# Branch moved to the fifth of eight expert pairs, gated-embedding products spaced evenly, one more weight tile, router products taken before LayerNorm

## The chip, the cores and the metric

One core of a Trainium2 chip runs the whole layer. The metric is the device time of one execution in microseconds, lower is better. Five engines work side by side, each on its own instructions in program order: TensorE (PE), VectorE (DVE), ScalarE (ACT), GpSimd (POOL), and SyncE (SP), which here issues every DMA.

## The reference, cut to what matters

One layer on 256 tokens of width 2048: a token-mixing part, a LayerNorm, a router, a mixture of 16 experts (two per token), a gated embedding, and a second LayerNorm. The part around the change is:

```python
x = _layer_norm(ALPHA * x + mix, ln1_g, ln1_b)
logits = xf @ router_w                      # 2048 x 16
affinity = sigmoid(logits); sel = affinity + router_bias
# best group of four experts, in it the best two
hb = silu(xb @ w_gate[e]) * (xb @ w_up[e]);  y = hb @ w_down[e]
ple = sigmoid(x @ ple_w_gate) * (p @ ple_w_proj)
x = _layer_norm(ALPHA * x + ffn + ple, ln2_g, ln2_b)
```

With LayerNorm written as x1 = (y - mean) * r, the logits are r * (y @ (g w)) - r * mean * (column sums of g w) + (column sums of b w). The changed router uses this form.

## The kernel before, in words

**Staging.** Everything is fp32 and every weight is read once. A pool of twelve tiles of 2 MB (128 x 4096 fp32, `big`, line 40) holds the weight stream and the large activations. `load_one` (line 127) issues one weight tile on SP; `prefetch` (line 142) issues as long as live tiles plus `state["reserve"]` stay below twelve, and `done` (line 152), called after the last product of a tile, frees that tile and calls `prefetch`. So a weight load waits on SP for the release of a tile, and SP issues in program order. `keep(n)` raises the reserve, `BR` takes a reserved tile for an activation. The small tiles come from a pool of five (`S`, line 55, 128 x 512 fp32); all of them carry one tag and are given out again in the order in which they came free.

**Order of the work.** The order is written out by hand. Short pieces of background work sit in a list `bg`; `pop_bg` (line 159) takes one after every second piece of a projection and one after every half tile of an expert product.

**Projections.** Until about 608 us each weight tile is split into a high and a low part (ACT line 264, DVE line 265) through four buffers, three pieces ahead of PE, and PE multiplies three times (line 283). The last of them are the four blocks of the output projection `wo` (line 510), each of 16 pieces. After each block DVE adds the residual (line 514) and takes LayerNorm statistics (line 515).

**Router.** After the last block: mean and deviation (lines 522 to 525, 553), a product of router weights and LayerNorm bias (line 565) and ten filler products `busy(10)` (line 567) on PE; then x1 is normalized in place by `norm_d` (DVE, line 557) and `norm_a` (ACT, line 561), turned by PE (line 578), copied out (lines 581, 583) and multiplied by the router weights (line 550). The logits are copied (line 601), turned (line 605), summed (line 608), and then come the sigmoid (line 611), the choice of experts (lines 613 to 648), the one-hot selection (line 676), the gather of the chosen rows (line 698) and the first expert product (line 790).

**Experts.** Eight pairs of experts, 64 places each. Each pair has phases A and B (8 tiles each, `inner`, line 806: gate and up products, line 790) and 0 and 1 (4 tiles each, `outer`, line 817: down products, line 797). `evac` (line 847) splits the result of an outer phase into four small tiles, yh on ACT and yl on DVE for each of two halves, and `scatter` (line 861) multiplies them by the selection and adds to `acc`. The scatters of phase 0 run as events after half tiles 1 to 4 of phase 1, and those of phase 1 in phase A of the next pair. The gathers for the next pair run as background, mostly in phase A.

**Gated embedding.** Eight products `ple(i)` (line 760) of 64 matmuls with one weight tile each, placed by the table `PLE` (line 31) after a phase of a pair. While one runs, PE releases no other tile.

**Branch.** `overflow` (line 927) holds a run-time branch (line 929) whose body, for experts with more than 64 tokens, is not entered with these inputs. It stands before phase A of the eighth pair. Two tiles are reserved for its body.

**Ends.** In the seventh pair the second LayerNorm's gain and bias are read into a tile `rows` (line 1010), spread over the partitions by two POOL broadcasts (lines 1026, 1027) into `gb2`, and also kept as two rows (line 1030). After the last expert product, line 1050 and following: statistics, six products of two rows with 512 columns (line 1072), a DVE operation for each (line 1073), and the stores.

Of the kernel before, what the change touches and what calls it, by code (L numbers as in the profile page):

```python
# [17 lines left out]
T = 256  # L18
# [12 lines left out]
PLE = [(2, "A"), (2, "1"), (3, "A"), (4, "A"), (4, "1"), (5, "A"), (6, "A"), (6, "B")]  # L31
# [3 lines left out]
def trunk(ctx, tc, I, out):  # L35
# [89 lines left out]
    wpt = C("wpt", [128, 2, 2, 256])  # L125

    def load_one():
# [8 lines left out]
        if key[0] == "ple":  # L136
            SP.dma_start(wpt[:, key[1] % 2], I["ple_w_proj"][key[1]])
# [63 lines left out]
    tail = C("tail", [128, 128])  # L201
    DVE.tensor_scalar(tail, jp, 0.0, None, op0=OP.is_le)
    capm = C("capm", [128, 128])
# [4 lines left out]
    ones = C("ones", [128, 128])  # L208
# [294 lines left out]
    rbias = C("rbias", [128, 1])  # L503
    DVE.memset(rbias, 0.0)
# [48 lines left out]
    DVE.scalar_tensor_tensor(lnm, lmv[:, :, 0], -1.0, lrs, op0=OP.mult, op1=OP.mult)  # L553

# [18 lines left out]
    for pr in range(8):  # L573
# [27 lines left out]
    DVE.tensor_scalar(lt[:, 0:256], rps[:, 0:256], rbias, None, op0=OP.add)  # L601
    busy(2)
    lg = AUX()
    for a in range(2):
# [4 lines left out]
                      op=OP.add)  # L609
    aff = r3("aff", 2, NE)  # L610
    ACT.activation(aff, logit, AF.Sigmoid)
    sel = r3("sel", 2, NE)
# [53 lines left out]
    long = {}  # L666
# [3 lines left out]
    hTs = [C(f"hT{k}", [128, 4, 128]) for k in range(2)]  # L670
    pT = C("pT", [128, 2, T])
    SP.dma_start(pT, I["pT"])
# [87 lines left out]
    def ple(i):  # L760
# [4 lines left out]
        for a in range(2):  # L765
            for c in range(2):
                PE.matmul(pw[:, a * 256:(a + 1) * 256], pT[:, c, a * 128:(a + 1) * 128], wpt[:, i % 2, c, :],
                          start=(c == 0), stop=(c == 1))
# [11 lines left out]
        if i == len(PLE) - 1:  # L780
            free()
            keep()
# [108 lines left out]
    rowc = C("rowc", [2, T])  # L891
# [35 lines left out]
    def overflow():  # L927
        most = nc.values_load(cmi[0:1, 0:1], min_val=0, max_val=T)
        with tc.If(most > CAP):
            with tc.For_i(0, NP, 1) as g:  # L930
# [5 lines left out]
                xg = B("og")[:, 0:2048].rearrange("p (c s) -> p c s", c=DC)  # L936
                with tc.For_i(1, T // CAP, 1):
                    DVE.tensor_scalar(ce[:, 0], ce[:, 0], -float(CAP), None, op0=OP.add)
                    P = Pm[:, 0]
                    onehot(P, ce[:, 0])  # L940
                    selection(P, ce[:, 1], 0, NP)
                    for f in gathers(P, xg):
                        f()
# [14 lines left out]
                    for k in range(2):  # L958
# [3 lines left out]
                        for f in scatters(evac(ps), 0, 1024 * k):  # L962
                            f()
                free(2)

    onehot(Pm[:, 0], pair_of(pos, 0))
    gather(Pm[:, 0], xgs[:, 0], 0)
    gather(Pm[:, 0], xgs[:, 0], 1)
    weights()
    bg.extend([lambda cp=cp: gather(Pm[:, 0], xgs[:, 0], cp) for cp in range(2, 8)])  # L970
    bg.append(lambda: selection(Pm[:, 0], pair_of(wA, 0), 0, 0))
    gb2 = rows = None
# [7 lines left out]
    for g in range(NP):  # L980
        xg, i = xgs[:, g % 2], g % 2
        following = []
        if g < NP - 1:
            P = Pm[:, 1 - i]
            following.append(lambda P=P, g=g: onehot(P, pair_of(pos, g + 1)))
            if g == 0:
                following.extend([lambda P=P, x=xgs[:, 1], cp=cp: gather(P, x, cp) for cp in range(8)])
            else:
                following.extend(gathers(P, xgs[:, 1 - i]))
# [8 lines left out]
        if g == 2:  # L998
            bg.extend([lambda q=q, a=a: residual(q, a) for q in range(4) for a in range(2)])
        if g == NP - 2:  # L1000
            keep()
        if g == NP - 1:
# [3 lines left out]
            keep(-2)  # L1006
            overflow()
        ps = inner("A", g, xg, events(back, 1))
        if g == NP - 2:
# [6 lines left out]
        ps = inner("B", g, xg, {3: lambda: turn_hidden(s, hTs[0])})  # L1016
        s = hidden(ps, g)
        ples(g, "B")
        if g == 0:
            bg.extend(following)  # L1020
# [3 lines left out]
        if g == NP - 2:  # L1024
            gb2 = BR("gb2")
            POOL.partition_broadcast(gb2[:, 0:2048], rows[0:1, 0:D], channels=128)
            POOL.partition_broadcast(gb2[:, 2048:2560], rows[0:1, 2 * D - 512:2 * D], channels=128)
# [3 lines left out]
            free()  # L1031
            keep()
# [31 lines left out]
    for a in range(2):  # L1064
        PE.matmul(ps[0:2, a * 128:(a + 1) * 128], cw[:, a, :], ident, start=True, stop=True)  # L1065
    ACT.activation(rowc, ps[0:2, 0:T], AF.Copy)  # L1066
# [3 lines left out]
    for n, (q, a) in enumerate((q, a) for q in range(3) for a in range(2)):  # L1070
        ps = (AUX, MM)[n % 2]()
# [67 lines left out]
```

## Time and profile before

| | |
|---|---|
| three timed runs, us | 1609.93, 1611.82, 1611.93 (median 1611.82) |
| the profiled execution, us | 1613.37 |
| its span from first to last instruction, us | 1611.7 |
| granted clock of TensorE, mean | 0.994 |
| busy share of the span | PE 97%, DVE 34%, ACT 25%, POOL 2% |
| moved by DMA | 540.08 MB, mean 335 GB/s |

The profiled execution lies 1.55 us above the median of the timed runs. A busy PE in these views is not PE at its peak, since the ends of matmuls are modelled; the share and rate of the DMA engines are those of the 16 engines together. "SPq" is the issuing side of SyncE and "PEq" that of TensorE. A granted clock of 1.00 is 2.4 GHz and one of 0.50 is 1.2 GHz.

### The profile page before, as it was taken

The numbers are of one execution on the slowest core, as the hardware profiler recorded it, in microseconds if no ns is written. First come the engines' busy times: TensorE is split into PE (matmuls) and PEld (weight loads), VectorE is DVE, ScalarE is ACT, GpSimd is POOL, SyncE is SP. The second block draws the span as 40 slices with busy tenths as digits, with TensorE's granted clock in tenths as the row PEclk, the third lists the DMA queues.
The fourth block names the chain that finished last, engine by engine and source line by source line (L and its number), as shares of the span: only waits on it lengthen the run. The fifth ranks groups of instructions, "written<-read, shape, count | busy, mean of one in ns | idle before, by whom it ended". The sixth has DMA issues, their size and how long they took to land. (4 is left out here: it accounts for less than half of the span.)

```text
span 1611.7 us, 17489 instructions
## 1 busy us (share of the span) xinstructions
PE 1571.3 (97%) x7226; PEld 910.5 (56%) x7226; DVE 546.9 (34%) x945; ACT 405.7 (25%) x714; POOL 37.8 (2%) x42
## 2 busy tenths in 40 slices
PE   8999999999999999999999999999999999998878
PEld 6888878888888885333334444533525533552323
DVE  5555575556565564022222112012011112101005
ACT  5455555455554442011111001001000101000000
POOL 0000000000000000000000000000000000000002
PEclk9999999999999999999999999999999999999998
DMA  9843453445546847999999999999999999999994
GB/s 383 346 157 111 182 205 147 178 160 207 186 180 263 336 188 274 416 428 427 427 428 425 414 426 429 382 428 428 427 428 427 418 429 427 427 427 389 416 429 197
DMA packets 43613, 540.08 MB, mean 335 GB/s; under 512 B 7172, under 2 KB 7172, under 8 KB 10758
## 3 DMA queue, kind: packets, MB, share of 16 engines
q1 hardware_dynamic: 43528, 538.91, 81.3%
q8 instruction: 58, 0.95, 0.3%
q14 instruction: 27, 0.22, 0.0%
HBM read 536.80 MB, written 2.10 MB: 334 GB/s over the span
## 5 line engine op out<-in xcount | busy, mean ns | idle before, releaser
L790 PE MATMUL mm<-w,xg 128*64 128x512 f32 x2048 | 467.7, 601 | 16.0 <-DMA w<-in_exp_w_dram 9.5
L283 PE MATMUL mm<-pc,xh 128*128 128x512 f32 x1152 | 362.9, 395 | 6.2 <-ACT pc L264 5.6
L265 DVE TENSOR_TENSOR pc<-w,pc 128x512 fp32r<-128x512 f32 x416 | 290.8, 709 | 199.6 <-ACT pc L264 196.9
L264 ACT ACTIVATE pc<-w 128x512 fp32r<-128x512 f32 x416 | 259.6, 630 | 234.0 <-DVE pc L265 179.7
L790 PEld LDWEIGHTS mm<-w,xg 128*64 128x64 f32 x2048 | 138.4, 137 | 277.1 <-issue 252.4
L797 PE MATMUL mm<-w,hT 128*64 128x512 f32 (+2 forms) x1088 | 236.2, 573 | 9.3 <-DMA w<-in_exp_d_last_dram 5.6
L283 PEld LDWEIGHTS mm<-pc,xh 128*128 128x128 f32 x1152 | 213.8, 189 | 51.8 <-ACT pc L264 6.0
L283 PE MATMUL mm<-pc,xl 128*128 128x512 f32 x576 | 225.4, 391 | 0.0
L797 PEld LDWEIGHTS mm<-w,hT 128*64 128x64 f32 x1088 | 72.5, 136 | 137.9 <-issue 127.4
L283 PEld LDWEIGHTS mm<-pc,xl 128*128 128x128 f32 x576 | 108.5, 188 | 22.9
L772 PE MATMUL mm<-w,x1T 128*128 128x256 f32 x512 | 112.0, 379 | 0.0
L772 PEld LDWEIGHTS mm<-w,x1T 128*128 128x128 f32 x512 | 97.2, 190 | 13.2
L834 DVE TENSOR_TENSOR s<-s,mm 128x256 f32<-128x256 f32 x32 | 13.3, 417 | 214.1 <-ACT s L833 214.1
L283 PE MATMUL mm<-pc,mixh 128*128 128x512 f32 x256 | 79.1, 390 | 0.0
L833 ACT ACTIVATE s<-mm 128x256 f32<-128x256 f32 x32 | 12.3, 384 | 235.1 <-PE mm L790 225.7
L873 DVE TENSOR_TENSOR acc<-acc,aux 128x512 f32<-128x512 f32 (+2 forms) x60 | 38.8, 650 | 94.4 <-PE aux L868 92.5
L855 ACT ACTIVATE yh<-mm 128x512 fp32r<-128x512 f32 (+1 forms) x32 | 18.5, 590 | 161.9 <-PE mm L797 161.9
L283 PEld LDWEIGHTS mm<-pc,mixh 128*128 128x128 f32 x256 | 47.9, 188 | 9.9
L283 PE MATMUL mm<-pc,mixl 128*128 128x512 f32 x128 | 49.8, 389 | 0.0
L856 DVE TENSOR_TENSOR yl<-mm,yh 128x512 fp32r<-128x512 f32 (+1 forms) x32 | 21.5, 682 | 82.1 <-ACT yh L855 81.9
L283 PE MATMUL mm<-pc,yax 128*128 128x512 f32 x192 | 44.2, 389 | 0.0
L283 PE MATMUL mm<-pc,obx 128*128 128x512 f32 x192 | 44.2, 389 | 0.0
(208 smaller groups left out, 835.0 us busy)
## 6 DMA issues: line engine op xcount, KB each, us to landing
w<-in_exp_w_dram SPq DMA_DIRECT2D x184, 2048.0 KB, 19.0
w<-in_w_in_dram SPq DMA_DIRECT2D x34, 2048.0 KB, 8.5
w<-in_w_o_dram SPq DMA_DIRECT2D x8, 2048.0 KB, 13.3
w<-in_ple_w_gate_dram SPq DMA_DIRECT2D x8, 2048.0 KB, 21.0
w<-in_exp_d_last_dram SPq DMA_DIRECT2D x7, 2048.0 KB, 39.1
w<-in_w_out_a_dram SPq DMA_DIRECT2D x4, 2048.0 KB, 8.1
w<-in_w_out_b_dram SPq DMA_DIRECT2D x4, 2048.0 KB, 7.9
w<-in_w_in_dram SPq DMA_DIRECT2D x3, 1024.0 KB, 10.9
```

Source lines behind the costliest of these rows:

```text
L264: ACT.activation(hi, w, AF.Copy)
L265: DVE.tensor_sub(lo, w, hi.bitcast(F32))
L283: PE.matmul(ps[a], l[:, c, as_], r, start=(first and n == 0), stop=(last and n == 2))
L772: PE.matmul(ps[:, a * 256:(a + 1) * 256], x1T[:, c, a * 128:(a + 1) * 128], w[:, c, :], start=(c == 0 and a == 0), stop=(c == DC - 1), ski ...
L790: PE.matmul(ps[k][es, :], x[:, es], w[:, e, k, :], start=(c == 0), stop=(c == DC - 1), skip_group_check=True, tile_position=(0, 64 * e))
L797: PE.matmul(p[es, 0:n], hTs[fc // 4][:, fc % 4, es], w[:, e, b * n:(b + 1) * n], start=(fc == 0), stop=(fc == 7), skip_group_check=True, t ...
L833: ACT.activation(s[:, ks], pg[:, ks], AF.Sigmoid)
L834: DVE.tensor_mul(s[:, ks], s[:, ks], pg[:, ks])
L855: ACT.activation(h, p[:, 0:n], AF.Copy)
L856: DVE.tensor_sub(l, p[:, 0:n], h.bitcast(F32))
L873: DVE.tensor_add(xb, xb, ps[:, 0:n])
```

## The change

Six parts. **The router** works on rows that are not normalized: x1 is turned right after the last block, the statistics of the last block and the deviation are taken meanwhile, and mean and deviation enter on the logits, two small DVE operations. The sums that this needs come from `column_sums`, background work in the fourth block: two products and two sums on DVE, one product on PE, a copy on DVE. The bias product and `busy(10)` go; x1 is normalized later, partly behind the logits. **The tiles:** the first pair's gathered rows move to memory of their own, so that eleven instead of ten tiles are free for weights in the router stage; the second gather buffer, the embedding's small weights, `pT` and `rowc` share one tile `late`, which is reserved in phase B of the first pair. **The embedding products** behind 3A, 5A and 6B go behind 3B, 5B and phase 1 of pair 6 (pairs counted from 0), so that 16 tiles lie between any two. **The branch** goes from before pair 7 to before pair 4, with one reserved tile. **The gain and bias** of the second LayerNorm are read without the tile `rows`: their last 512 columns go into small tiles `ends`, from which POOL spreads them; the two tiles of the split x1 are freed in pair 6. **At the end** a filler product follows each of the first five two-row products.

```diff
-PLE = [(2, "A"), (2, "1"), (3, "A"), (4, "A"), (4, "1"), (5, "A"), (6, "A"), (6, "B")]
+PLE = [(2, "A"), (2, "1"), (3, "B"), (4, "A"), (4, "1"), (5, "B"), (6, "A"), (6, "1")]
+OVER = 4
...
+            SP.dma_start(long["wp"][:, key[1] % 2], I["ple_w_proj"][key[1]])
...
+    red = C("red", [128, 2, NE])
+    rsb = C("rsb", [128, 2, NE])
     lst = C("lst", [128, 2, 4, 6])
     lmv = C("lmv", [128, 2, 2])
     lrs = C("lrs", [128, 2])
     lnm = C("lnm", [128, 2])
+    def column_sums():
+        rwb = S("rwb").rearrange("p (c e) -> p c e", c=DC)
+        for k, t in ((0, rwg), (1, rwb)):
+            DVE.tensor_tensor(t, rw, gc[:, k, :, None].to_broadcast([128, DC, 32]), op=OP.mult)
+            DVE.tensor_reduce(red[:, k], t.rearrange("p c e -> p e c")[:, 0:NE, :], axis=AX.X, op=OP.add)
+        ps = AUX()
+        PE.matmul(ps[:, 0:2 * NE], ones, red.rearrange("p k e -> p (k e)"), start=True, stop=True)
+        DVE.tensor_copy(rsb.rearrange("p k e -> p (k e)"), ps[:, 0:2 * NE])
+    def stats(i, a):
+        DVE.bn_stats(lst[:, a, i, :], x1[:, a, i * 512:(i + 1) * 512])
...
+        if i == 3:
+            bg.extend([None, column_sums])
...
-            DVE.bn_stats(lst[:, a, i, :], xb)
-        if i == 2:
-            DVE.tensor_tensor(rwg, rw, gc[:, 0, :, None].to_broadcast([128, DC, 32]), op=OP.mult)
+            if i < 3:
+                stats(i, a)
     free(3)
-    xgs = B("xg").rearrange("p (h c s) -> p h c s", h=2, c=DC)
+    xgs = [C("xg0", [128, DC, 128]), None]
     prefetch()
-    for a in range(2):
-        DVE.bn_aggr(lmv[:, a, :], lst[:, a, :, :])
-    DVE.tensor_scalar(lrs, lmv[:, :, 1], EPS, None, op0=OP.add)
-    POOL.tensor_tensor(lrs, lrs, half, op=OP.pow)
+    def scales():
+        for a in range(2):
+            DVE.bn_aggr(lmv[:, a, :], lst[:, a, :, :])
+        DVE.tensor_scalar(lrs, lmv[:, :, 1], EPS, None, op0=OP.add)
+        POOL.tensor_tensor(lrs, lrs, half, op=OP.pow)
...
-    rbp = AUX()
-    for c in range(DC):
-        PE.matmul(rbp[0:32, 0:1], rw[:, c, :], gc[:, 1, c:c + 1], start=(c == 0), stop=(c == DC - 1))
-    DVE.tensor_copy(rbias[0:32, :], rbp[0:32, 0:1])
-    busy(10)
-    norm_d(0, 0)
-    norm_a(0, 1)
-    norm_d(1, 0)
-    norm_a(1, 1)
...
-        if pr == 1:
-            norm_d(2, 0)
-            norm_a(2, 1)
-        if pr == 3:
-            norm_d(3, 0)
-            norm_d(3, 1)
-        if pr % 2 == 1 and pr > 1:
-            route_mm(pr - 3, xts[pr - 3])
+    for pr in range(8):
+        turn_raw(pr)
+        if pr in (1, 3):
+            stats(3, pr // 2)
+        if pr == 5:
+            scales()
+        if pr >= 2:
             route_mm(pr - 2, xts[pr - 2])
     route_mm(6, xts[6])
     route_mm(7, xts[7])
+    DVE.scalar_tensor_tensor(lnm, lmv[:, :, 0], -1.0, lrs, op0=OP.mult, op1=OP.mult)
+    for a in range(2):
+        DVE.scalar_tensor_tensor(red[:, a], rsb[:, 0], lnm[:, a:a + 1], rsb[:, 1], op0=OP.mult, op1=OP.add)
+    norm_d(0, 0)
+    for q, a in ((0, 1), (1, 0), (1, 1)):
+        norm_a(q, a)
...
-    DVE.tensor_scalar(lt[:, 0:256], rps[:, 0:256], rbias, None, op0=OP.add)
+    DVE.tensor_copy(lt[:, 0:256], rps[:, 0:256])
+    norm_d(2, 0)
...
+        DVE.scalar_tensor_tensor(logit[:, a], logit[:, a], lrs[:, a:a + 1], red[:, a], op0=OP.mult, op1=OP.add)
     aff = r3("aff", 2, NE)
     ACT.activation(aff, logit, AF.Sigmoid)
+    for q, a in ((2, 1), (3, 0), (3, 1)):
+        norm_a(q, a)
...
-    pT = C("pT", [128, 2, T])
-    SP.dma_start(pT, I["pT"])
+    hTs = [hT0, C("hT1", [128, 4, 128])]
+    def take_late():
+        t = BR("late")
+        xgs[1] = t[:, 0:2048].rearrange("p (c s) -> p c s", c=DC)
+        long["wp"] = t[:, 2048:3072].rearrange("p (k c f) -> p k c f", k=2, c=2)
+        long["pT"] = t[:, 3072:3584].rearrange("p (c t) -> p c t", c=2)
+        long["rowc"] = t[0:2, 3584:3840]
+        SP.dma_start(long["pT"], I["pT"])
...
-                xg = B("og")[:, 0:2048].rearrange("p (c s) -> p c s", c=DC)
+                xg, f = xgs[1 - OVER % 2], 1 - OVER % 2
...
+        if g == OVER - 1:
+            bg.extend([None] * 20 + [keep])
         if g == NP - 2:
-            keep()
-        if g == NP - 1:
+            bg.append(lambda: (free(2), keep()))
+        if g == OVER:
             for f in back:
                 f()
             back = []
-            keep(-2)
+            keep(-1)
             overflow()
         ps = inner("A", g, xg, events(back, 1))
...
-            rows = BR("rows")
-            SP.dma_start(rows[0:1, 0:D], I["ln2_g"])
-            SP.dma_start(rows[0:1, D:2 * D], I["ln2_b"])
-            keep()
...
+        ps = inner("B", g, xg, {3: lambda: turn_hidden(s, hTs[0]), **({11: keep} if g == 0 else {})})
...
+            take_late()
...
             gb2 = BR("gb2")
-            POOL.partition_broadcast(gb2[:, 0:2048], rows[0:1, 0:D], channels=128)
-            POOL.partition_broadcast(gb2[:, 2048:2560], rows[0:1, 2 * D - 512:2 * D], channels=128)
             gbr = gb2[0:2, 2560:4096]
             for k, r in enumerate((I["ln2_g"], I["ln2_b"])):
                 SP.dma_start(gb2[k:k + 1, 2560:4096], r[:, 0:1536])
-            free()
-            keep()
+                ends = S("ends")
+                SP.dma_start(ends[0:1, :], r[:, 1536:2048])
+                POOL.partition_broadcast(gb2[:, 1536 + 512 * k:2048 + 512 * k], ends[0:1, :], channels=128)
+            POOL.partition_broadcast(gb2[:, 0:1536], gb2[0:1, 2560:4096], channels=128)
         y = evac(ps)
...
-        ps = (AUX, MM)[n % 2]()
+        ps = MM()
         PE.matmul(ps, rowc[:, a * 128:(a + 1) * 128], gbr[:, q * 512:(q + 1) * 512], start=True, stop=True)
+        if n < 5:
+            busy(1)
```

## Rows read from the trace of the kernel before

**Rows 1.** The page, 40 equal slices, busy tenths of the DMA engines.

```profile
DMA  9843453445546847999999999999999999999994
```

**Rows 2.** The chain that ended last, in order of time: start, us, what.

```profile
1498.98 34.42 DMA w<-in_exp_w_dram
...
1533.47 39.10 DMA w<-in_exp_d_last_dram
...
1572.70 1.94 PE mm L797 x8
```

**Rows 3.** Stretches: us, busy of each engine, granted clock, DMA share, GB/s.

```profile
621.00:632.00 11.00, 10.35 (x63) 5.81 (x61) 4.99 (x28) 1.37 (x3) 0.00 (x0) 1.00 0.03 10
...
652.00:893.00 241.00, 241.00 (x1119) 95.17 (x1116) 52.48 (x107) 32.71 (x69) 0.00 (x0) 1.00 1.01 428
893.00:905.00 12.00, 12.00 (x61) 5.38 (x59) 3.36 (x5) 0.60 (x1) 1.27 (x1) 1.00 0.96 373
...
1024.00:1034.00 10.00, 10.00 (x47) 5.97 (x47) 0.69 (x1) 0.60 (x1) 1.27 (x1) 1.00 0.67 252
...
1484.00:1496.00 12.00, 12.00 (x50) 4.26 (x48) 0.00 (x0) 0.00 (x0) 0.00 (x0) 0.85 0.70 264
```

**Rows 4.** PE in order of time, an undisturbed phase of pair 0.

```profile
675.63 14.76 PE L790 MATMUL mm<-w,xg 128*64 128x512 f32 x68
```

**Rows 5.** SP's waits over the span: us in total, times, longest.

```profile
SPq L135 <- PE mm L772: 124.3, 8, 16.5
```

**Rows 6.** The router's stage in order of time: start us, us, what.

```profile
607.80 1.17 PE L565 MATMUL aux<-gc,rw 128*32 128x1 f32 x32
...
612.00 2.20 PE L578 MATMUL mm<-ident,x 128*128 128x128 f32 x16 [0.77 <-DVE x L557]
...
618.91 0.48 DVE L601 TENSOR_SCALAR lt<-aux,rbias 128x256 f32<-128x256 f32 x1 [0.80 <-PE aux L550]
...
619.93 0.29 DVE L608 TENSOR_REDUCE logit<-aux 128x32 f32<-128x128 f32 x1 [0.53 <-PE aux L605]
...
626.21 1.94 PE L790 MATMUL mm<-w,xg 128*64 128x512 f32 x8
```

**Rows 7.** DVE at the start of the fourth block, in order of time.

```profile
588.70 0.67 DVE L517 TENSOR_TENSOR rwg<-rw,gc 128x512 f32<-128x512 f32 x1
```

**Rows 8.** The branch: PE in order of time, then stretches.

```profile
1482.40 17.83 PE L790 MATMUL mm<-w,xg 128*64 128x512 f32 x70 [6.53 <-PEq L929]
...
1482.00:1486.00 4.00, 3.60 (x10) 1.27 (x12) 0.00 (x0) 0.00 (x0) 0.00 (x0) 0.50 1.00 422
1486.00:1488.00 2.00, 2.00 (x8) 0.59 (x6) 0.00 (x0) 0.00 (x0) 0.00 (x0) 0.58 0.59 246
```

**Rows 9.** DMA issues at 648 and at 1144: KB, us to landing.

```profile
w<-in_exp_w_dram SPq DMA_DIRECT2D x1, 2048.0 KB, 7.6
...
w<-in_exp_w_dram SPq DMA_DIRECT2D x1, 2048.0 KB, 16.9
```

**Rows 10.** SP's issue of a gain row; packets 1453 to 1467, 1467 to 1468.

```profile
1453.03 0.25 SPq L1030 DMA_DIRECT2D gb<-in_ln_g_dram  x1
...
DMA packets 412, 6.00 MB, mean 429 GB/s; under 512 B 45, under 2 KB 45, under 8 KB 45
...
DMA packets 33, 0.44 MB, mean 438 GB/s; under 512 B 5, under 2 KB 5, under 8 KB 7
```

**Rows 11.** POOL's broadcast of 512 columns, in order of time.

```profile
1455.39 0.80 POOL L1027 PARTITION_BROADCAST gb<-rows  x1
```

**Rows 12.** The end: PE in order of time, then one stretch.

```profile
1593.83 3.62 PE L530 MATMUL aux<-ones_b 128*128 128x512 bf16 x16
...
1598.44 1.12 PE L1072 MATMUL aux<-gb,rowc 2*128 2x512 f32 x2 [0.46 <-ACT rowc L1066]
...
1605.34 1.91 PE L1072 MATMUL mm<-gb,rowc 2*128 2x512 f32 x2
...
1600.00:1602.00 2.00, 2.00 (x4) 0.71 (x4) 1.10 (x2) 0.00 (x0) 0.00 (x0) 0.58 0.37 135
```

More of the change, by code (lines that the diff above doesn't have):

```diff
@@ L123, in BR @@
         return B(name, dt)
-    wpt = C("wpt", [128, 2, 2, 256])
+    long = {}
     def load_one():
@@ L551, in route_mm @@
                       stop=(c >= 12), skip_group_check=True, tile_position=(0, 32 * g))
-    DVE.scalar_tensor_tensor(lnm, lmv[:, :, 0], -1.0, lrs, op0=OP.mult, op1=OP.mult)
     def norm_d(q, a):
@@ L561, in norm_a, with turn_raw @@
         ACT.activation(xb, xb, AF.Identity, scale=lrs[:, a:a + 1], bias=lnm[:, a:a + 1])
-    rbp = AUX()
-    for c in range(DC):
-        PE.matmul(rbp[0:32, 0:1], rw[:, c, :], gc[:, 1, c:c + 1], start=(c == 0), stop=(c == DC - 1))
-    DVE.tensor_copy(rbias[0:32, :], rbp[0:32, 0:1])
-    busy(10)
-    norm_d(0, 0)
-    norm_a(0, 1)
-    norm_d(1, 0)
-    norm_a(1, 1)
     xts = {}
-    for pr in range(8):
+    def turn_raw(pr):
         ps = MM()
@@ L609, in trunk @@
                       op=OP.add)
+    for a in range(2):
+        DVE.scalar_tensor_tensor(logit[:, a], logit[:, a], lrs[:, a:a + 1], red[:, a], op0=OP.mult, op1=OP.add)
     aff = r3("aff", 2, NE)
     ACT.activation(aff, logit, AF.Sigmoid)
+    for q, a in ((2, 1), (3, 0), (3, 1)):
+        norm_a(q, a)
     sel = r3("sel", 2, NE)
@@ L663, in weights @@
         DVE.tensor_copy(cmi, cmax)
-    long = {}
     Pm = C("Pm", [128, 2, 2, 128], F32R)
@@ L766, in ple @@
             for c in range(2):
-                PE.matmul(pw[:, a * 256:(a + 1) * 256], pT[:, c, a * 128:(a + 1) * 128], wpt[:, i % 2, c, :],
+                PE.matmul(pw[:, a * 256:(a + 1) * 256], long["pT"][:, c, a * 128:(a + 1) * 128], long["wp"][:, i % 2, c, :],
                           start=(c == 0), stop=(c == 1))
@@ L935, in overflow @@
                 ow = B("ow").rearrange("p (k f) -> p k f", k=2)
-                xg = B("og")[:, 0:2048].rearrange("p (c s) -> p c s", c=DC)
+                xg, f = xgs[1 - OVER % 2], 1 - OVER % 2
                 with tc.For_i(1, T // CAP, 1):
                     DVE.tensor_scalar(ce[:, 0], ce[:, 0], -float(CAP), None, op0=OP.add)
-                    P = Pm[:, 0]
+                    P = Pm[:, f]
                     onehot(P, ce[:, 0])
-                    selection(P, ce[:, 1], 0, NP)
-                    for f in gathers(P, xg):
-                        f()
+                    selection(P, ce[:, 1], f, NP)
+                    for fn in gathers(P, xg):
+                        fn()
                     n = 0
@@ L961, in overflow @@
                             mm_d(ps, row(16 + 4 * k, fc).rearrange("p (e f) -> p e f", e=2), fc)
-                        for f in scatters(evac(ps), 0, 1024 * k):
-                            f()
-                free(2)
+                        for fn in scatters(evac(ps), f, 1024 * k):
+                            fn()
+                free()
     onehot(Pm[:, 0], pair_of(pos, 0))
-    gather(Pm[:, 0], xgs[:, 0], 0)
-    gather(Pm[:, 0], xgs[:, 0], 1)
+    gather(Pm[:, 0], xgs[0], 0)
+    gather(Pm[:, 0], xgs[0], 1)
     weights()
-    bg.extend([lambda cp=cp: gather(Pm[:, 0], xgs[:, 0], cp) for cp in range(2, 8)])
+    bg.extend([lambda cp=cp: gather(Pm[:, 0], xgs[0], cp) for cp in range(2, 8)])
     bg.append(lambda: selection(Pm[:, 0], pair_of(wA, 0), 0, 0))
-    gb2 = rows = None
+    gb2 = None
     back = []
@@ L980, in trunk @@
     for g in range(NP):
[L981 removed]
+        xg, i = xgs[g % 2], g % 2
         following = []
@@ L986, in trunk @@
             if g == 0:
-                following.extend([lambda P=P, x=xgs[:, 1], cp=cp: gather(P, x, cp) for cp in range(8)])
+                following.extend([lambda P=P, cp=cp: gather(P, xgs[1], cp) for cp in range(8)])
             else:
-                following.extend(gathers(P, xgs[:, 1 - i]))
+                following.extend(gathers(P, xgs[1 - i]))
             following.append(lambda P=P, g=g, i=i: selection(P, pair_of(wA, g + 1), 1 - i, g + 1))
@@ L1065, in trunk @@
         PE.matmul(ps[0:2, a * 128:(a + 1) * 128], cw[:, a, :], ident, start=True, stop=True)
+    rowc = long["rowc"]
     ACT.activation(rowc, ps[0:2, 0:T], AF.Copy)
```

15 lines of the change are left out of this document (4 added, 11 removed).

## The prediction, made before the change was run

> **What bounds the kernel now.** I read the slices of the span first [rows 1]: the 16 DMA engines are far from full until about slice 16 (645 us) and full from there to the last slice but two. The chain that ended last [rows 2] says the same of the end: it is made of weight loads, each waiting behind the loads ahead of it (34.4 and 39.1 us from issue to landing), until one lands at 1572.6; what follows, 39.1 us to the end of the span, is PE and the closing operations. So the time is the moment at which the weight stream has delivered that tile, plus an end of 39 us. The stretches [rows 3] show where the stream loses time: a tile of 2.097 MB at 428 GB/s takes 4.9 us, and the stream stands at that rate except in 621 to 632 (share 0.03, no free tile while the router works), 893 to 905 (0.04 of 12 us, 0.5), 1024 to 1034 (0.33 of 10, 3.3) and 1484 to 1496 (0.30 of 12, 3.6). PE is the second bound: a tile costs it 14.76/68 x 16 = 3.5 us where nothing else runs [rows 4], 1.4 less than the stream needs, but while an embedding product runs no other tile comes free: SP waits 124.3/8 = 15.5 us for each of the eight [rows 5]. Where fewer than that are queued, the stream runs dry, and its restart is then set by PE alone.
>
> **The change, part by part.**
>
> *Router.* Before, PE is through with the blocks at 607.8 and the first transpose starts at 612.0, after statistics and norm; the turning and multiplying last until 618.7, the logits are copied at 618.9, and the first expert product starts at 626.2 [rows 6]. After, the turning starts at 607.8: 4.2 us removed, with the bias product (1.2 us) and the fillers inside that gap. Back come, ahead of the copy, one normalization of a quarter, the two small sums and lnm, and behind it two small operations on the logits: I put 1.8 on these, by analogy with 0.48 for the copy and 0.29 for the reduction. That leaves 2.4 us. Against it stand the column sums in the fourth block: two products of 0.67 [rows 7] and two reductions of twice the 128 elements that take 0.29 [rows 6], about 0.4 each, so 2.2 us on DVE, and a PE product that stands in PE's order after the fourth piece. DVE can only begin when it has split the seventh piece, whose buffer the third piece frees, which is when the fourth is nearly done; PE then waits for nearly all of it, 2.4 with the product. Net 0; between -2.4 (the sums wholly covered) and +1.
>
> *Eleven tiles.* One more load, 4.9 us, goes into the idle 621 to 632 [rows 3]. It does not last: the lead is bounded by the tiles that PE releases, from phase B of the first pair the number of tiles is that of before, and at 893 to 905 the stream is already dry for 0.5. With 4.9 more lead it is dry there for about 5, and restarts when PE is through with that embedding product, at the same time as before. Net 0; bounds 0 and -0.5.
>
> *Embedding products spaced.* The loss at 1024 to 1034 lies at the product behind 3A, 8 tiles after another one. Behind 3B PE has gained 8 x 1.4 = 11 us on the stream first, more than the 3.3 that are missing. -3.3; bounds 0 and -3.6 with the small dip at 5A.
>
> *Branch.* Before, PE stands still for 6.5 us there and then works at 1.2 GHz (granted 0.50) until about 1487.6 [rows 8], 5.2 us at half rate or 2.6 lost. The stream runs empty, since nothing new is issued until all that is under way has landed, and loses 3.6. That is the price of the branch wherever the stream is the bound, so moved to pair 4 it costs the same: 0. But 8 tiles later comes the embedding product behind 4A. Before, the load issued after it took 16.9 us to land, against 7.6 for one that finds nothing queued [rows 9], a margin of 9.3; the branch takes 6.5 + 2.6 = 9.1 of PE's time just ahead. So it is used up: +1, between 0 and the 3.3 that the product behind 3A cost.
>
> *Gain and bias.* This decides the sign. The broadcasts now read tiles `ends` from the pool of five. After them `evac` takes four more (yh, yl, yh, yl), so the fourth gets the memory of the first `ends`, and DVE's second yl waits for POOL's broadcast of it, which waits for its load. PE meets this as the third scatter in phase 1 of pair 6 and stops, since it works in order; everything of pair 6 and 7 is queued behind it. And the load is late: before, a row issued by SP at 1453.0 found the stream ahead of it; of packets between 2 and 8 KB none moved up to 1467 and two between 1467 and 1468 [rows 10], 14.4 us later, with five tiles for the stream. After, eight are free there (twelve less `late`, `acc`, x1T and `gb2`), so up to 14.4 + 3 x 4.9 = 29 us. PE reaches the third scatter some 9 us after the issue and stands for about 20. What the stream loses follows from the landing L of `ends`: only two tiles were released in between, so after L it has loads for 9.8 us. PE goes on at L + 0.8 (broadcast [rows 11]) + 0.7 (yl, like other DVE work of its size) + 0.4 for the waits = L + 1.9, at half clock as after the branch (2.6 lost [rows 8]), with four scatter matmuls of 0.23 (from the fillers [rows 12]: 3.62/16) and one tile, 3.5: next release at L + 8.9, landing at 8.9 + 7.6 = 16.5 where 14.7 was due: 1.8 lost. The tile after it comes 3.5 later and lands in turn at 21.4; then the embedding product now placed there holds all releases for 15.5, until L + 27.9, and the next landing is at 35.5 instead of 26.3: 9.2 lost. Together +11.0. It depends little on how long PE stands; bounds 0 (the load lands before PE needs it) and 13 (PE, left behind by 20 us, ends after the stream).
>
> *End.* Six two-row products start between 1598.44 and 1605.34, the last taking 1.9 [rows 12]: PE falls to half clock in them. With a filler after each and the clock kept, a step is 0.86 + 0.23 = 1.1, the last starts at 1603.9 and takes 1.0: -2.3. If the clock falls in spite of it, from the third on a step is 1.7 + 0.45: +1.6. The rows show products of two rows back to back (PE busy 2.00 of 2.00) and the granted clock at 0.58 all the same, whereas the full-height fillers ahead of them, from 1593.83, ran at full clock. I take -2.3, since what is added is of that second kind. The Trainium skill (TensorE: Matmul & The Clock Gate, section "HAM oscillation") has it that the clock is kept where PE has no long idle gaps; by that rule the clock would not have fallen here before. The trace does not agree; by the rule the term is still -2.3, by the row alone +1.6.
>
> *Sum:* router 0, tiles 0, spacing -3.3, branch 0 + 1, gain and bias +11.0, end -2.3: +6.4. On the profiled execution 1613.4 + 6.4 = 1619.8; the median of the runs lies 1.55 below it, so 1611.8 + 6.4 = **1618.2 us**.
>
> **The rivals.**
>
> *The small loads hold up nothing (chance 0.29).* If the second yl gets other memory than that of `ends`, or if the 2 KB come past the queue, the term of 11 goes and -4.6 is left: 1607.2, faster. For it: the pool's order is read from the code, no row shows it. Against: the row of 14.4 us [rows 10]. The point that decides is one wait, DVE's second yl in pair 6.
>
> *The clock falls at the end (0.17).* As priced: +1.6 instead of -2.3, the sum +10.3: 1622.1. For it the 0.58 [rows 12].
>
> *The column sums are covered (0.12).* If PE does not wait for DVE in the fourth block, the 2.4 of the router stay, and since the dry spot at 893 is set by PE they go through to the end: +4.0, 1615.8. This is also the case in which the router does what its form says; in my forecast the shorter router is not seen in the time.
>
> The forecast itself has 0.42.
>
> **How the numbers follow.** 0.2%, or 3.2 us, is about what a measurement of this kernel can tell from no change: faster is below 1608.6, slower above 1615.0. The first rival lies 1.4 below the lower bound, with the branch term (0 to 3.3) and the router (-2.4 to +1) open: 0.24 of its 0.29 faster, 0.05 same. Of the three slower cases, 0.71, I count 0.11 as same, where the term of 11 is a few us smaller, and 0.02 as faster. So faster 0.26, same 0.16, slower 0.58. The range reaches from 1605.5, which takes in most of the first rival, to 1624.5, above the second; the likeliest case alone has 1614 to 1622.
>
> **What would show it.** Right: a wait of PE of 15 to 30 us in phase 1 of pair 6, ended by DVE's yl, with POOL's broadcast just before; a clock of 0.50 after it; the DMA share below 1 for some 10 us at the last embedding product; no dip at the product behind 3B; a dip of some 5 us near 893 and one of 3 to 4 at the branch before pair 4; a wait of PE for DVE of 2 us in the fourth block; first expert product within 1 us of 626; the two-row products 1.1 us apart. Wrong: a second yl of pair 6 that follows its yh at once, which alone turns the sign; a lead from the eleventh tile that is still there after 905; a loss of more than 4 us at 4A.

## The result, and the profile after

| | before | after |
|---|---|---|
| median of the runs, us | 1610.95 (1609.93 to 1611.93, 4 runs) | 1626.54 (1626.25 to 1627.56, 4 runs) |
| profiled execution, its span | 1613.37, 1611.7 | 1626.40, 1624.7 |
| start of the 16 fillers behind the last tile | 1593.83 [rows 12] | 1603.29 |
| first two-row product to start of the last DVE operation | 8.85 (1598.44 to 1607.29) | 12.41 (1607.90 to 1620.31) |

The change is slower: 15.6 us between the medians, ratio 1.0098 (95% interval 1.0080 to 1.0115). Between the two spans it is 13.0: 9.46 until the last fillers start, 3.56 in the products behind them. The other 2.6 us lie outside the two profiles: that of before took 2.4 us more than the median of its runs, that of after 0.1 less. The sign and the wait named as decisive were right; 1626.5 lies 2.0 above the top of the range.

The page after: DMA and clock in 40 slices, and the share of the chain that ended last by engine.

```profile
PEclk9999999999999999999999999999999999996998
...
DMA  9843454354556848999999999998999999999893
...
PE 26%; DMA 5%; DVE 0%; POOL 0%; issue 0%; ACT 0%; SPq 0%
```

A slice of lost transfers now stands at the branch (the 28th), the clock falls near 1480, and the end of the chain is mostly PE, where before it was weight loads [rows 2].

**The end rows.** POOL, DVE and PE after, in order of time (start, us, operation, in brackets the idle time before and what ended it), then one stretch (us, busy of each engine, clock, DMA share, GB/s).

```profile
1480.54 1.48 POOL L1053 PARTITION_BROADCAST gb<-ends  x2 [76.13 <-DMA w<-in_exp_w_dram]
1481.38 0.69 DVE L881 TENSOR_TENSOR yl<-mm,yh 128x512 fp32r<-128x512 f32 x1 [34.09 <-POOL gb L1053]
...
1482.12 0.80 PE L893 MATMUL aux<-yl,PO 128*128 128x512 f32 x1 [24.46 <-DVE yl L881]
...
1482.85 3.68 PE L822 MATMUL mm<-w,hT 128*64 128x512 f32 x8
...
1488.00:1512.00 24.00, 24.00 (x112) 16.06 (x108) 2.48 (x4) 1.79 (x3) 1.27 (x1) 1.00 0.61 233
```

The second `yl` of pair 6 waits for POOL's broadcast of the end row whose memory it takes, and PE for that `yl`: 24.46 us. Then eight products take 3.68 us that take 1.94 elsewhere (half clock), and the stream loses 0.39 of 24 us, 9.4.

**The router's stage.** PE after, in order of time, with one stretch at the place of the wait; then one row of PE before.

```profile
593.71 0.61 PE L519 MATMUL aux<-red,hT 128*128 128x32 f32 x2 [2.61 <-DVE red L517]
594.13 1.20 PE L286 MATMUL mm<-pc,mixh 128*128 128x512 f32 x2
...
611.89 1.47 PE L587 MATMUL mm<-ident,x 128*128 128x128 f32 x12
613.30 0.62 PE L567 MATMUL aux<-xt,rwg 128*32 128x256 f32 x4
613.86 0.66 PE L587 MATMUL mm<-ident,x 128*128 128x128 f32 x4
614.44 0.63 PE L567 MATMUL aux<-xt,rwg 128*32 128x256 f32 x4
...
620.42 0.60 PE L547 MATMUL aux<-ones_b 128*128 128x512 bf16 x2
...
628.31 1.08 PE L815 MATMUL mm<-w,xg 128*64 128x512 f32 x4
...
594.00:597.00 3.00, 3.00 (x9) 2.42 (x9) 0.79 (x2) 0.00 (x0) 0.00 (x0) 0.50 0.39 82
```

```profile
614.13 0.64 PE L550 MATMUL aux<-xt,rwg 128*32 128x256 f32 x8
```

PE waits 2.61 us for the column sums, and the clock is 0.50 behind the wait; the blocks end at 611.89, not 607.80. Four products with the router's weights now take the time of eight before (0.62 and 0.64), so turning and multiplying lasts 8.5 us (to 620.42) where it lasted 6.7. The first expert product starts 2.1 us later than before [rows 6], and every tile up to pair 3 stands 2.11 us later.

**The stretches** after (as above), and PE at the branch.

```profile
893.00:899.00 6.00, 6.00 (x31) 4.10 (x29) 1.29 (x2) 0.60 (x1) 0.17 (x1) 1.00 0.51 156
1024.00:1034.00 10.00, 10.00 (x50) 3.42 (x48) 0.00 (x0) 0.00 (x0) 0.00 (x0) 1.00 1.00 421
1106.00:1114.00 8.00, 8.00 (x36) 3.22 (x36) 1.10 (x2) 1.17 (x3) 0.00 (x0) 1.00 0.46 154
...
1099.82 6.49 PE L815 MATMUL mm<-w,xg 128*64 128x512 f32 x16 [6.12 <-PEq L953]
```

The dry stretch near 895 has grown from 0.5 us [rows 3] to 3, the one at 1024 to 1034 is gone, the branch costs the stream 4.3 (0.54 of 8; 3.6 before).

**The end.** PE after, in order of time, then one stretch.

```profile
1607.90 1.12 PE L1095 MATMUL mm<-gb,late 2*128 2x512 f32 x2 [0.46 <-ACT late L1089]
1608.95 0.39 PE L547 MATMUL aux<-ones_b 128*128 128x512 bf16 x1
1609.27 1.12 PE L1095 MATMUL mm<-gb,late 2*128 2x512 f32 x2
...
1610.64 2.00 PE L1095 MATMUL mm<-gb,late 2*128 2x512 f32 x2
1612.58 0.61 PE L547 MATMUL aux<-ones_b 128*128 128x512 bf16 x1
...
1612.00:1618.00 6.00, 6.00 (x8) 1.30 (x7) 1.73 (x3) 0.00 (x0) 0.00 (x0) 0.50 0.34 131
```

The clock falls in the third product, fillers or not. A step takes 1.37 us at full clock and 2.5 at half, not the 1.1 and 2.15 of the prediction.

### The profile page after: what moved, and what is told of

Read it like the earlier page. It is cut to its first block, busy times and chain, and to the rows that moved or that the text cites. A ratio compares the mean times of both kernels' runs of the same rounds, so it can differ in the third digit from the quotient of the medians.

```text
span 1624.7 us, 17427 instructions
## 1 busy us (share of the span) xinstructions
PE 1575.2 (97%) x7191; PEld 910.7 (56%) x7191; DVE 548.2 (34%) x948; ACT 407.9 (25%) x717; POOL 37.9 (2%) x43
## 5 line engine op out<-in xcount | busy, mean ns | idle before, releaser
L815 PE MATMUL mm<-w,xg 128*64 128x512 f32 x1024 | 235.3, 604 | 6.1 <-PEq L953 6.1
L815 PE MATMUL mm<-w,late 128*64 128x512 f32 x1024 | 231.0, 597 | 0.0
L815 PEld LDWEIGHTS mm<-w,xg 128*64 128x64 f32 x1024 | 69.4, 138 | 135.1 <-issue 127.1
L815 PEld LDWEIGHTS mm<-w,late 128*64 128x64 f32 x1024 | 69.0, 136 | 131.0 <-issue 130.4
L859 DVE TENSOR_TENSOR s<-s,mm 128x256 f32<-128x256 f32 x32 | 13.4, 418 | 194.5 <-ACT s L858 194.5
```

The lines of the kernel that those rows point to most:

```text
L815: PE.matmul(ps[k][es, :], x[:, es], w[:, e, k, :], start=(c == 0), stop=(c == DC - 1), skip_group_check=True, tile_position=(0, 64 * e))
```

## The experiments

Times are compared with runs of the kernel before on the same chip; the median of before was 1611.87 for e1 to e4, 1611.73 for e5, e8, e10, e11, 1612.23 for e6, e12 to e14, and 1613.22 for e15 and e16. Since the moment of the clock's fall at the end shifts a time by some us, each reading also goes by the start of the last fillers ("fillers", 1603.29 after). Four kernels that are the same up to there but for two fills with zeros (after, e2, e6, e16) have them between 1600.12 and 1603.29, so a difference of less than some 3 us between two single profiles shows nothing by itself.

**e1.**

```diff
-                ends = S("ends")
...
+                ends = gb2[0:1, 512 * k:512 * k + 512]
...
```

> The kernel after with one edit: the two end rows of gain and bias are read into memory of gb2 that is written last (columns 0 to 1023 of partition 0), so no tile of the pool of five is taken; the same four small loads, the same three broadcasts. Theory (the wait on the tiles of the end rows is what costs): DVE's second yl of pair 6 follows its yh at once, PE's wait of 24.5 us in phase 1 of pair 6 and the half clock behind it are gone, the stream no longer loses its 9.5 us between 1488 and 1512, and the time falls by about 9.5, from 1626.5 to about 1617. Rival (the four small loads take the places of weight loads in SP's queue, which alone empties the stream): the wait goes but half or more of the 9.5 us stays, 1621 or more, and the transfers still stand still near the last embedding product.

Measured 1614.92 (1611.28 to 1616.34, 10 runs), ratio to before 1.0016 (1.0007 to 1.0026); fillers at 1592.89, 10.4 earlier. PE and POOL of e1, then the stretch that lost 9.4 us after:

```profile
1457.90 0.50 PE L893 MATMUL aux<-yh,PO 128*128 128x512 f32 x1
1458.24 0.40 PE L893 MATMUL aux<-yl,PO 128*128 128x512 f32 x1
...
1481.26 1.48 POOL L1053 PARTITION_BROADCAST gb<-gb  x2 [74.53 <-DMA gb<-in_ln_b_dram]
...
1488.00:1512.00 24.00, 24.00 (x106) 7.87 (x106) 2.75 (x4) 0.00 (x0) 1.26 (x1) 1.00 1.00 425
```

The end rows land as late as after (broadcast at 1481.26), but the third scatter runs on at 1457.90 and the stream loses nothing. The theory holds; the four small loads themselves cost nothing, so the rival is out.

**e2** and **e6**, the fillers.

```diff
         if n < 5:
-            busy(1)
+            busy(4)
```

(e6; in e2 both lines go.)

> The kernel after without the filler product behind each of the first five two-row products at the end. Theory (the clock falls in these products with fillers and without, so a filler only adds its own time): from the first two-row product to the start of the last DVE operation 12.4 us become 8.9 as in the kernel before, and the time falls by 3.5, to 1623.0. Rival 1 (the fillers keep the clock for a product or two): less than half of that, 1625 or more. Rival 2 (as predicted, the fillers keep the clock and are worth 2.3): the end gets longer, 1628 or more.

> The kernel after with four fillers instead of one behind each of the first five products at the end. Theory (products of full height between them keep the clock if there are enough): granted clock at full speed to the end, a step of 2.06 us, the last DVE operation 11.6 us behind the first product instead of 12.4: 1625.7. Rival (the clock falls all the same): steps of 3.9 us from the third or fourth on, 16 to 18 us behind the first product, 1630 to 1632.

e2: 1618.86 (1617.20 to 1622.45, 4 runs), fillers at 1602.33. e6: 1630.63 (1628.85 to 1634.30, 4 runs). The six products of e2 with the stretches there, then e6's third group of fillers and a stretch:

```profile
1606.94 5.84 PE L1095 MATMUL mm<-gb,late 2*128 2x512 f32 x12 [0.46 <-ACT late L1089]
...
1604.00:1612.00 8.00, 7.54 (x26) 3.08 (x23) 6.27 (x11) 0.37 (x1) 1.17 (x1) 0.99 0.43 156
1612.00:1618.00 6.00, 0.79 (x1) 0.00 (x0) 1.03 (x2) 0.00 (x0) 0.00 (x0) 0.50 0.46 143
```

```profile
1612.28 1.89 PE L547 MATMUL aux<-ones_b 128*128 128x512 bf16 x4
1614.09 2.07 PE L1095 MATMUL mm<-gb,late 2*128 2x512 f32 x2
...
1612.00:1618.00 6.00, 6.00 (x12) 1.45 (x11) 1.50 (x2) 0.00 (x0) 0.00 (x0) 0.52 0.25 96
```

More fillers do not keep the clock: e6 takes 16.66 us from the first product to the last DVE start, as its rival said. Without any, e2's profile is through in 5.88: the clock falls only in the sixth product, whose second half runs at 0.50. No theory had that. Its runs spread over 5.3 us where after's spread over 1.3, and the moment of the fall differs from profile to profile: in 13 of the 14 with two-row products it lies between the second and the fourth product, in e2 in the sixth. From the first product to the last DVE start the seven with one filler take 10.5 to 13.4 us, the six with none 5.9 to 8.9. So the fillers cost time, and in no profile do they keep the clock.

**e3.**

```diff
...
-            bg.extend([None, column_sums])
+            bg.extend([None, lambda: times(0, rwg), lambda: sums(0, rwg), lambda: times(1, rwb), lambda: sums(1, rwb), None,
+                       over_rows])
...
-        if pr >= 2:
-            route_mm(pr - 2, xts[pr - 2])
+        if pr % 2 == 1 and pr > 1:
+            route_mm(pr - 3, xts[pr - 3])
+            route_mm(pr - 2, xts[pr - 2])
```

(The edit also takes `column_sums` apart into the three functions `times`, `sums` and `over_rows`.)

> The kernel after with two edits in the router stage. The two products and two reductions of the column sums are queued one at a time behind every second piece of the fourth block, and PE's product over the rows two places later; and the products with the router's weights are issued four at a time again, as before, not two. Theory: PE's wait of 2.6 us for the sums and the lower clock behind it (1.4) go, the turning and multiplying takes 6.7 us as before instead of 8.5, so the first expert product starts at about 622.5 instead of 628.3. The time follows only as far as the dry spot of the stream near 895 (3.2 us of idle transfers) allows: -3, 1623.5. Rival 1 (the dry spot is the stream's own): the stage gets shorter by 5.8 and the time stays at 1626.5. Rival 2 (all of it goes through): 1620.7.

Measured 1620.35 (1620.10 to 1620.58, 4 runs), fillers at 1596.71, 6.6 earlier. PE of e3:

```profile
607.78 1.91 PE L592 MATMUL mm<-ident,x 128*128 128x128 f32 x16
609.62 0.64 PE L572 MATMUL aux<-xt,rwg 128*32 128x256 f32 x8
...
614.22 0.60 PE L552 MATMUL aux<-ones_b 128*128 128x512 bf16 x2
...
622.11 1.94 PE L821 MATMUL mm<-w,xg 128*64 128x512 f32 x8
```

The stage is shorter by what was expected: the wait and the half clock behind it are gone (607.78), the loop takes 6.4 us, the first expert product starts 6.2 earlier. But all of it reaches the end, as rival 2 said: the expert tiles start 6.2 us earlier at the first and 6.6 at the last, and the dry stretch, now at 887 to 893, is no shorter (4.0 us, after 3.5). PE sets the restart, so PE's time goes through however dry the stream is.

**e4** and **e10**, the branch left out ahead of pair 4 (of after) and ahead of pair 7 (of before).

```diff
-            keep(-1)
-            overflow()
```

(e4; its reservation in pair 3 goes too. e10 leaves out the call alone.)

> The kernel after with the overflow branch and its reservation left out: the work for a pair of experts with more than 64 rows is not there. It prices the branch where it stands now. Theory (the branch costs the transfers it stops, 4.3 us between 1106 and 1114, and they are carried to the end): 1622.2. Rival 1 (PE's stand there is absorbed, since PE has slack behind it and the end is set by PE's later wait): 1626. Rival 2 (PE's 10.9 us are carried too, since PE ends behind the stream): 1616 to 1618.

> The kernel before with the overflow branch left out (the work for a pair of experts with more than 64 rows is not there), its reserved tiles left as they are. It prices the branch where it stood, for comparison with the price of 4.3 to 5.7 us at its new place. Theory (the branch costs what the stream loses, 3.6 us near 1490): 3.6 us faster than before, so that the move by itself costs 1 to 2. Rival 1 (PE's 9.1 us are in the end too): 6 or more. Rival 2 (PE has time in hand there): 0.

e4: 1620.80 (1618.41 to 1622.29, 4 runs), fillers 5.0 earlier, and nothing is lost at 1106 to 1114. That is theory within the spread. e10: 1609.08 (1607.11 to 1611.30, 10 runs), ratio 0.9981 (0.9972 to 0.9991), fillers only 1.7 earlier than before, since this run lost 1.9 us near 1284, where before lost 0.3; without that it is 3.3. So the branch costs about 5 at its new place and about 3 at the old one.

**e5.**

```diff
-PLE = [(2, "A"), (2, "1"), (3, "A"), (4, "A"), (4, "1"), (5, "A"), (6, "A"), (6, "B")]
+PLE = [(2, "A"), (2, "1"), (3, "B"), (4, "A"), (4, "1"), (5, "B"), (6, "A"), (6, "B")]
```

> The kernel before with two entries of the table of embedding products changed alone: the third moves from behind phase A to behind phase B of pair 3, the sixth likewise in pair 5. Theory (the two dry stretches go, 3.3 us near 1030 and 0.3 near 1282, and nothing later gives it back): the start of the fillers behind the last tile comes 3.4 us earlier, and the time falls by 3.4 from the median of before. Rival (the stream, being ahead, runs dry later instead, at the branch or at the last products): less than 1 us.

Measured 1608.19 (1607.12 to 1609.21, 10 runs), ratio 0.9976 (0.9967 to 0.9985): 3.5 us faster, fillers 3.6 earlier. Theory.

**e11, e12, e15**, ten tiles.

```diff
     xgs = [C("xg0", [128, DC, 128]), None]
+    late = B("late")
     prefetch()
+    SP.dma_start(late[:, 3072:3584], I["pT"].rearrange("p c t -> p (c t)"))
...
-        t = BR("late")
+        t = late
...
-        SP.dma_start(long["pT"], I["pT"])
```

(e15. All three also leave out the reservation in phase B. e12 has the load of pT where it was; e11 has `keep()` in place of the tile.)

> The kernel after with the eleventh tile held back in the router stage (one tile reserved from the end of the blocks on, and the reservation in phase B of the first pair left out), so that from that phase on both have the same tiles. Theory (the lead is lost where the stream runs dry near 895, since PE sets the restart there): the dry spot near 895 is shorter by 3 us or more, everything behind it stands at the same place within 0.5 us, and the time is 1626.5 within 1.5. Rival (the eleventh tile is worth a load's time): 4.9 us slower, 1631.

> The kernel after with the eleventh tile really held: the tile `late` is allocated in the router stage, where the kernel before took its tile for the gathered rows, instead of in the first pair's phase 0, and the reservation in phase B goes. (In e11 a reservation without a tile held nothing back: the fourth load behind the blocks was issued at 611.45 all the same.) Theory (the lead of the eleventh tile is what is lost in the dry spot near 895, since PE sets the restart): the dry spot there falls from 3.5 us to 0.5 or less, PE's tiles behind it stand where they stood within 0.7 us, time 1626.5 within 1.5. Rival 1 (the tile is worth its load): 4.9 us slower, 1631. Rival 2 (the dry spot has another cause): 3.5 us are idle there still.

> e12 with the load of pT into the tile `late` right behind the loads of the router stage. (In e12 too the fourth load behind the blocks was issued at once, at 611.03: a tile takes its memory at its first use, not where it is allocated. Now its first use stands ahead of that load.) Theory (the eleventh tile's lead is what is lost in the dry spot near 895): that load waits for PE's first release, at about 632; the dry spot falls from 3.5 us to 0.7 or less; PE's tiles behind it stand within 0.7 us of where they stood, relative to the first expert product; the time is 1625.5 within 2. Rival 1 (the tile is worth its load): 1630 or more. Rival 2 (the dry spot has another cause): 3.5 us idle there still.

e11: 1625.82, e12: 1624.61 (4 runs each); in both the tile went to a load all the same, so they test nothing; the dry stretch was 3.9 and 4.1 us. e15: 1626.38 (1623.34 to 1627.55, 4 runs). Its stretches:

```profile
628.00:636.00 8.00, 8.00 (x48) 4.31 (x48) 2.42 (x10) 1.83 (x4) 0.00 (x0) 1.00 0.17 33
893.00:899.00 6.00, 6.00 (x31) 4.73 (x31) 0.72 (x2) 0.60 (x1) 0.00 (x0) 1.00 1.01 421
```

With ten tiles really held the stream idles some 5 us longer around the router and not at all near 895, and the time is the same. The eleventh tile moves an idle stretch, as predicted.

**e8**, the edits of e1, e2 and e3 in one kernel; **e13** and **e14** start from it.

> The kernel after with three edits together: the end rows in memory of gb2, no fillers between the two-row products, and both edits of the router stage. Theory (each removes a loss at a place of its own: 10.4, 1.0 to 7.5 with the clock's fall as it comes, and 6.2 measured singly): the fillers behind the last tile start 16.5 us earlier than in after, the stream is without idle at the last embedding product, and the time is 1602 to 1606, below both kernels. Rival (with PE no longer behind, the stream sets the end and takes back the router's 6): 1608 or more.

Measured 1604.01 (1602.86 to 1605.78, 5 runs), ratio 0.9953 (0.9939 to 0.9966); fillers at 1586.37, 16.9 earlier than after. Theory: the losses are separate and add.

```diff
-OVER = 4
+OVER = 7
...
         if i == len(PLE) - 1:
             free()
+            keep()
...
-                free()
+                free(3)
...
-            bg.extend([None] * 20 + [keep])
+            pass
...
-            bg.append(lambda: (free(2), keep()))
+            bg.append(keep)
```

> e8 with the overflow branch back ahead of pair 7, and with what it needs there: the two tiles of the split rows stay to the branch, and the tile of x1T goes to it. Theory (singly, leaving the branch out gave 5.0 to 5.7 us ahead of pair 4 and 2.7 ahead of pair 7): 2 to 3 us faster than e8, 1601 to 1602. Rival (the two tiles fewer in pair 6 make the stream run dry at the last two embedding products): 1604 or more.

Measured 1605.44 (1604.21 to 1606.49, 4 runs), fillers at 1587.93, 1.6 later than e8. The 2 to 3 us of the theory did not come. The time is the rival's, but not its cause: the stream is not idle at the last two embedding products, it loses 5.4 us at the branch against 4.2 in e8. The ranges of the two kernels overlap, so which place is better in this setting is not shown.

**e14** and **e16**, full height.

```diff
-        long["rowc"] = t[0:2, 3584:3840]
+        long["rowc"] = t[:, 3584:3840]
+        POOL.memset(long["rowc"], 0.0)
...
-            gbr = gb2[0:2, 2560:4096]
+            gbr = gb2[:, 2560:4096]
+            POOL.memset(gbr, 0.0)
...
-    ACT.activation(rowc, ps[0:2, 0:T], AF.Copy)
+    ACT.activation(rowc[0:2], ps[0:2, 0:T], AF.Copy)
```

> e8 with the products at the end 128 rows high instead of two (both operands hold zeros in the other 126 rows). Theory (what keeps the clock is how many rows of the array work, as the prediction took it of the fillers): the clock stays, six products take 5.8 us as in e2, the last DVE operation starts 7.0 us or less behind the first product instead of 8.7, and the time is 1601 to 1602, with a small spread. Rival (the height has no part in it): the clock falls in the third or fourth product as in e8, 1604 within 1.

> The kernel after, its fillers too, with the products at the end 128 rows high instead of two (zeros in the other 126). Theory (the rows at work keep the clock, as e14's profile showed once): full clock to the end, a step of 1.37 us throughout, the last DVE operation 8.0 us behind the first product instead of 12.4, and the time 4.4 us shorter, 1622.0. Rival (e14's full clock was the moment of the fall, which changes from run to run, as in e2): the clock falls between the second and the fourth product as in after, 1625 to 1627.

e14: 1602.29 (1601.61 to 1603.22, 4 runs). e16: 1618.95 (1617.43 to 1620.65, 7 runs). PE of e14 with one stretch, then PE and stretches of e16, its fourth block first:

```profile
1590.83 5.39 PE L1103 MATMUL mm<-gb,late 128*128 128x512 f32 x12 [0.56 <-ACT late L1097]
...
1590.00:1596.00 6.00, 5.45 (x15) 2.20 (x12) 4.19 (x6) 0.37 (x1) 0.00 (x0) 1.00 0.60 214
```

```profile
593.88 0.38 PE L519 MATMUL aux<-red,hT 128*128 128x32 f32 x2 [2.61 <-DVE red L517]
594.00:597.00 3.00, 3.00 (x15) 2.49 (x16) 1.36 (x3) 0.63 (x1) 0.00 (x0) 1.00 0.46 98
...
1605.97 1.02 PE L1097 MATMUL mm<-gb,late 128*128 128x512 f32 x2
1606.83 0.38 PE L547 MATMUL aux<-ones_b 128*128 128x512 bf16 x1
1607.05 1.02 PE L1097 MATMUL mm<-gb,late 128*128 128x512 f32 x2
...
1610.27 1.02 PE L1097 MATMUL mm<-gb,late 128*128 128x512 f32 x2
...
1604.00:1612.00 8.00, 6.74 (x20) 2.68 (x17) 5.00 (x7) 0.37 (x1) 0.00 (x0) 1.00 0.54 203
```

Both profiles keep the full clock until the last product is through, and in e16 the step is 1.07 us, less than expected: a filler behind a product of its own height starts 0.86 after it, behind one of two rows 1.05. From first product to last DVE start e16 takes 6.5 us against 12.4. The theory holds in both. Of the 7.6 us that e16 gains on after, these 5.9 belong to it. In its profile the fillers start 3.2 us earlier too, 1.3 of them because the wait of 2.61 us in the fourth block is not followed by half clock there.

**The version that beats both** is e14: 9.9 us, or 0.6%, below before (1612.23), ratio 0.9940 (0.9923 to 0.9957).

## Why the prediction was right or wrong

| term, us | predicted | measured | from |
|---|---|---|---|
| router | 0 | +2.1 | first expert product, 628.31 and 626.21 |
| eleven tiles | 0 | 0 | e15 |
| spacing | -3.3 | -3.5 | e5 |
| branch | 0 + 1 | +0.5 | what is left of the 9.46 at the fillers |
| gain and bias | +11.0 | +10.4 | e1 |
| end | -2.3 | +3.6 | 12.41 and 8.85 |
| sum | +6.4 | +13.1 | spans: +13.0 |

**Right: gain and bias.** The chain is the one described: `ends`, broadcast, `yl`, third scatter, half clock, then lost transfers at the embedding product behind it. PE stood 24.5 us, not 20; the stream lost 0.9 and 8.6 (predicted 1.8 and 9.2). That PE may end behind the stream was only a bound (13); it does, since the chain's end is PE now, but it adds just 1 us to the 9.4 lost.

**Right: spacing and eleven tiles**, in size and in mechanism (e5, e15); the dip near 893, foreseen at about 5 us, is 3.5. e3 shows the same rule from the other side: what PE gains ahead of the dry spot goes through.

**Right within its bounds: the branch.** The loss foreseen at the product behind 4A does not appear, no stretch there is below 1. In its place the branch itself costs the stream a little more (4.3, not 3.6). What the move alone does stays open between the two settings: e4 against e10 makes it some 2 us dearer, e13 shows no clear difference with the tiles counted in. The 0.5 is a remainder, not a run of its own, and smaller than what two profiles can tell; that it comes close to the +1 is no proof of the reasoning.

**Wrong: the router.** Two steps failed. "The turning and multiplying last until 618.7" was carried over as if the loop had not changed; but `route_mm` is issued for two pieces at a time, not four, which made 8.5 us of 6.7. Each piece's column group is its number modulo 4, so before, four groups worked side by side, and now two. The Trainium skill (TensorE: Matmul & The Clock Gate, "Part 3: Packing small matmuls — row/col tiling") says that products in different column groups of the array run at once; the rows agree, eight products in 0.64 us before, four in 0.62 after. The other step is "PE then waits for nearly all of it, 2.4 with the product": wait and product were 3.0, but behind the wait PE ran at half clock for 3 us, which I priced at the branch and not here, another 1.4. Against that, the small operations put at 1.8 cost 0.4: from the end of the loop to the first expert product it is 7.9 us after (620.42 to 628.31) and was 7.5 before (618.73 to 626.21). In sum 4.1 (blocks' end) + 1.8 + 0.4 - 4.2 = 2.1. The 1.4 is not there each time: the same wait of 2.61 us stands in nine profiles, and half clock goes with it in six. In the other three (e11, e12, e16) the first expert product starts at 626.62 to 627.04, 0.4 to 0.8 later than before.

**Wrong: the end.** "I take -2.3, since what is added is of that second kind": the row of 0.58 [rows 12] was read rightly and then set aside. The clock fell, so the rival's case held, and its size (+1.6) was too low as well: its steps were built from products that follow each other (0.86) plus a filler (0.23), while a filler and a two-row product do not overlap like that (1.37 together, 2.5 at half clock). In e16, where the products have full height, the step is 1.07, as its 1.1 had it. What was added was of the second kind, but the two-row products stayed what they were, and among them the clock fell in every profile.

These two steps, 2.1 and 5.9, make 8.0 of difference; the other terms take back 1.3, which leaves the 6.7 between the two sums. The measured median lies 8.3 above the forecast, not 6.7: the forecast went by the median of before, and 1.55 of this is how far the profile of before lay above it. The range failed for the same reason: the falling clock was in it, at too low a price and never together with the router's loss.

## What to carry to other kernels

A small tile taken from a rotating pool for data that land late hands its lateness to whoever gets the memory next; read in a buffer that is written last anyway, the same data cost nothing. Where a diff reorders a loop, count again how many of its products can work side by side, not only how many there are. Time that PE gains ahead of a dry spot of the stream counts, while a buffer's lead there does not, as long as PE sets the restart. Products of two rows are worth a padding with zeros to full height where the clock falls in them (5.9 us at the end of e16), and fillers behind them are not.

## What the runs showed of the hardware that was not expected

SP's queue after, in order of time:

```profile
1452.79 0.31 SPq L1050 DMA_DIRECT2D gb<-in_ln_g_dram  x1
1457.70 0.22 SPq L1052 DMA_DIRECT2D ends<-in_ln_g_dram  x1
1462.52 0.22 SPq L1050 DMA_DIRECT2D gb<-in_ln_b_dram  x1
1467.51 0.22 SPq L1052 DMA_DIRECT2D ends<-in_ln_b_dram  x1
```

The four small loads are not issued together: they stand 4.9 us apart, the time of one weight load. So the load of the first `ends` was issued 4.9 us after the first row. The same spacing in e1 cost nothing.

With two-row products and PE busy from the first of them on, the clock fell to half in all 14 profiles, with no filler, with one and with four of full height behind each (0.52 in e6). With 128 rows, mostly zeros, it stayed at 1.00 until the last product was through in the two profiles (e14, e16). The mean granted clock of the other runs agrees: 0.997 to 0.998 in the four runs of e14 against 0.993 to 0.996 in e8, and 0.988 to 0.990 in the seven of e16 against 0.983 to 0.985 in after.

The wait of 2.61 us in the fourth block went with a clock of 0.50 in six profiles (after, e1, e2, e4, e6, e15) and with none in three (e11, e12, e16). The Trainium skill (TensorE: Matmul & The Clock Gate, "HAM oscillation — how this bites in real kernels") tells of a clock lost to waits longer than this one; here it was lost six times with a shorter one, and at the end with no wait between the products.
